# Two-layer hybrid decoder on one core: rotary queries copied to unit stride, masks moved off TensorE, some divisions on ScalarE, a new order

## The chip, the core and the metric

The kernel runs on one core of a Trainium2 chip. The core has five engines with a queue each: TensorE (PE, with its weight loads shown apart as PEld), VectorE (DVE), ScalarE (ACT), GpSimd (POOL) and SyncE (SP, which here only starts DMAs). TensorE reads SBUF and writes the eight banks of PSUM; VectorE and ScalarE read both; GpSimd works on SBUF only. The engines run side by side and wait for one another on semaphores, and each takes its own queue strictly in the order in which the program was written.

The metric is the device time of one execution in microseconds. Three runs of the kernel before gave 275.26, 276.06 and 277.32 us, so the median is 276.06 us.

## The reference

Two layers work on `x`, 256 tokens of 1024 features in float32. Each normalises `x`, projects it to ten groups of columns, runs three kinds of heads, gates their outputs and projects them back:

```python
h = rms_norm(x, norm_g[layer])
proj = jnp.einsum('btd,dc->btc', h, w_in[layer])
sb_q, sb_k, sb_v, sb_g, mb_q, mb_k, mb_v, mb_g, mem_q, mem_g = jnp.split(proj, split_at, axis=-1)
o_sb  = stick_breaking_attention(sb_q, sb_k, sb_v) * silu(sb_g)      # 6 heads of 64
o_mb  = moba_attention(rotary(mb_q), rotary(mb_k), mb_v) * silu(mb_g) # 6 heads of 64
o_mem = memory_attention(mem_q, mk, mv) * silu(mem_g)                # 4 heads, 256 memory tokens
x = x + concat[o_sb, o_mb, o_mem] @ w_out[layer]
```

A stick-breaking head weighs key s for query t by `sigmoid(z_ts) * prod_{s<j<t} (1 - sigmoid(z_tj))` over strictly earlier keys. With 256 tokens the "moba" heads have a single block, so they are causal softmax attention after a rotary turn of the first 16 of 64 dimensions. The memory heads are softmax attention without a mask. A last `rms_norm` ends the program.

## The kernel before, in words

**Projections.** Every large product is made from three products of parts: a weight `raw` is split into `hi` (the value rounded to the type that TensorE reads quickly) and `lo = raw - hi`, and the activations likewise (`T`, `mxhi`, `mxlo`). The weights arrive in 111 chunks, 768 columns wide in the main, in five `raw` buffers; a chunk is turned into `hi` (L256 on ScalarE, now and then L277 on VectorE) and `lo` (L262 on VectorE), with seven buffers of each. SyncE starts the load of a chunk when the `lo` of five chunks before is written, so a late VectorE also means late loads.

**Heads.** Scores are plain float32 products on 64 rows, two heads side by side (`pair_scores`). The tiles are named `sb_q`, `sb_k`, `mem_q`, `mem_k`, and `uT` for the rotary heads: their queries lie in `uT[:, 0:3]`, their keys in `uT[:, 3:6]`. Rotary queries and keys are produced with tokens on the partitions, turned by four small VectorE operations (`rope_task`), transposed in 32x32 blocks on VectorE (`rope_turn`, L820) and then sent through DRAM and back (`trip`: one DMA `Z<-D`, four DMAs back), which finishes the transposition. The block transposition of the queries writes them so that in `uT` neighbouring query columns of one head pair stand six elements apart; the keys stand in runs of 32.

In `pair_scores` a causal mask is added on TensorE: after the scores of a stick-breaking or a rotary pair, the product of an identity (`identb`, bf16) with a table of 0 and -1e30 (`masks`, bf16) is accumulated into the two diagonal blocks of each head. `setup` makes both on GpSimd from a constant.

A stick-breaking head (`sb_head`) then takes a tanh on ScalarE, turns it into 1 - sigmoid (L258 ACT or L684 DVE), runs a scan over the keys from the last to the first (L687, multiply, then a maximum with a `carry` that holds the start value at the block borders), and multiplies (L266). A softmax head (`soft_head`) takes the row maximum of two regions from PSUM on VectorE (L702), the exponential with its sum from PSUM on ScalarE, a reciprocal (L711) and a division (L270), both on VectorE. All heads go through a block transposition (L732) and a trip, and `pair_task` multiplies them with the values on TensorE.

**What sets the order.** No engine order is written by hand. A planner in the kernel (`Sched`) holds tasks with a priority, an estimated cost of each operation and an estimated time at which each result is ready, and always issues the operation that can start earliest, by priority within a slack. `SCAN` is its estimate of the scan in ns per element; `URG` says how many chunks ahead of TensorE a `hi` or `lo` becomes urgent; `HOLD`, `SPARE2` steer how score products are gathered and how many PSUM banks they must leave free; `ORDER` is the order of the pieces of the projection in each layer.

Of the kernel before, what the change touches and what calls it, by code (L numbers as in the profile page):

```python
# [9 lines left out]
BF = mybir.dt.bfloat16  # L10
AF = mybir.ActivationFunctionType
OP = mybir.AluOpType
# [4 lines left out]
D = 1024  # L17
# [15 lines left out]
P_H0 = -8  # L33
P_RX = 1
P_M0 = 12
P_RM = 4
P_M1 = 4
URG = 2
X67_AT = 5
CST_AT = 6  # L40
X0_AT = 7
# [4 lines left out]
DMA_GBS_1K = 300.0  # L46
TRIP_LAT = 1500.0
MEM_AT = 1
ORDER = (["sb_qk", "mb_q", "mb_k", "mk", "mv", "mem_q", "mb_v", "sb_v", "mb_g", "sb_g", "mem_g"],
         ["mv", "mk", "mb_k", "mb_q", "sb_k", "sb_q", "sb_v", "mb_g", "mem_q", "mb_v", "sb_g", "mem_g"])  # L50
GATES = {"sb_g": 3, "mb_g": 3, "mem_g": 2}
HOLD = 6000.0
SPARE2 = 2
DVE_HI = 400.0
SLACK_PE = 60.0
SLACK = 120.0


# [141 lines left out]
def hybrid_trunk(ctx: ExitStack, tc: tile.TileContext, x, mem, norm_g, w_in, w_mem_kv, w_out,  # L200
# [12 lines left out]
        return ap.tensor.name.startswith("bank")  # L213

    mode = {"m": None}

    def pe_mode(m):

# [49 lines left out]

    def ts(out, a, s, op=OP.mult):
        nc.vector.tensor_scalar(out, a, s, None, op0=op)  # L270
        S.op("dve", 1.0417 * _free(out) + 65.0)

    def copy(out, in_, eng):
        if eng == "act":
# [13 lines left out]
    xs = sb("xs", [128, 2, D])  # L288
    cst = sb("cst", [128, 512])
    gc = sb("gc", [128, 32])  # L290
    identb = sb("identb", [128, 128], BF)
    masks = sb("masks", [128, 2, 128], BF)
    negone = sb("negone", [128, 128])
    junk = sb("junk", [128, 512], BF)
    gb = sb("gb", [128, D])
# [100 lines left out]
    def dma_chunk(now=0.0, q=None):  # L396
        j = prog["dma"]
        if j >= len(chunks):
            return
        p, kk, c, w = chunks[j]  # L400
        n = len(kk)
        dma(raws[j % RAW][:, :n * w].rearrange("p (k c) -> p k c", c=w),
            p.src[:, kk[0]:kk[0] + n, c:c + w], ("raw", j), q, now)
        prog["dma"] += 1
        if j == X67_AT:
            load_xT(6, 8, now=now)
        for t, at in enumerate((X0_AT, X1_AT)):
            if j == at:
                dma(xs[:, t, :], x_r[:, t, :], ("x", t), now=now)
        if j == CST_AT:  # L410
            dma(cst, consts[:, 0:512], "cst", now=now)
            dma(S.res["w"].items[0][2][:, :256], consts[:, 512:768], "msk", now=now)

    def hi_task():
        for j, (p, kk, _, w) in enumerate(chunks):
# [42 lines left out]
    def setup():  # L458
        yield R("pool")
        nc.gpsimd.memset(negone, -1.0)  # L460
        S.op("pool", 2400.0)
        S.mark("setup0")
        yield R("pool", need=["cst", "msk"])
        m = S.res["w"].items[0][2][:, :256]
        nc.gpsimd.tensor_copy(identb, ident)
        nc.gpsimd.tensor_copy(masks, m.rearrange("p (m c) -> p m c", m=2))
        nc.gpsimd.memset(carry, 0.0)
        nc.gpsimd.memset(carry[:, 128:129], 0.5)
        for _, _, a in S.res["a"].items:
            nc.gpsimd.memset(a[:, 384:385], 0.5)  # L470
        S.op("pool", 2400.0)
        S.mark("setup")

# [170 lines left out]
    def pair_scores(l, kind, c):  # L644


        qn, kn = {"sb": ("sb_q", "sb_k"), "mem": ("mem_q", "mk"), "mb": ("mb_q", "mb_k")}[kind]
        _, sc = yield R("pe", need=["setup", (qn, l, c), (kn, l, c)], alloc=["bank", "bank"],
                      spare=3, spare2=SPARE2, form="row")
        if kind == "mem":  # L650
            regs = [(slice(0, 256), slice(0, 128), slice(0, 256)), (slice(256, 512), slice(128, 256), slice(0, 256))]
        else:
            regs = [(slice(0, 128), slice(0, 128), slice(0, 128)), (slice(128, 384), slice(128, 256), slice(0, 256))]
        st, mv_ = qs[kind], ks[kind]
        for j, (o, a, b) in enumerate(regs):
            for h in range(2):
                r = slice(h * 64, h * 64 + 64)
                lhsT, rhs, out = st[r, c, a], mv_[r, c, b], sc[h][:, o]
                if kind == "mb":
                    lhsT = st.rearrange("p c x -> p (c x)").rearrange("p (n m) -> p m n", m=6)[r, 3 * j + c]  # L660
                    rhs = mv_.rearrange("p c x -> p (c x)").rearrange("p (i t c a) -> p c t i a", i=4, t=2, c=3)[r, c, 0:1 + j]
                    out = out.rearrange("p (t i a) -> p t i a", i=4, a=32)
                mm(out, lhsT, rhs, j == 0, kind == "mem" and j == 1)
        if kind != "mem":
            yield R("pe")
            for h in range(2):
                for j, o in enumerate((slice(0, 128), slice(256, 384))):
                    mm(sc[h][:, o], identb, masks[:, 0 if kind == "sb" else 1, :], False, j == 1)
        for h in range(2):
            S.mark(("qkdone", l, kind, 2 * c + h))  # L670
            scs[l, kind, 2 * c + h] = sc[h]

    def sb_head(l, h):


# [4 lines left out]
        e, (a,) = yield R(("act", 413.0), ("dve", 265.0), alloc=["a"])  # L680
        if e == "act":
            act(a[:, 0:384], w, AF.Copy, scale=-0.5, bias=0.5)
        else:
            nc.vector.tensor_scalar(a[:, 0:384], w, -0.5, 0.5, op0=OP.mult, op1=OP.add)  # L684
            S.op("dve", 0.52 * 384 + 65.0)
        yield R("dve")
        nc.vector.tensor_tensor_scan(a[:, 383::-1], a[:, 383::-1], carry[:, ::-1], 0.5, op0=OP.mult, op1=OP.max)  # L687
        S.op("dve", SCAN * 384 + 70.0)
        yield R("dve")
        stt(w, w, 1.0, a[:, 1:385], OP.add, OP.mult)  # L690
        S.free("a", a)
        S.mark(("w", l, "sb", h))
        ws[l, "sb", h] = w

    def soft_head(l, h, kind):
        mb = kind == "mb"
        first = 0 if mb else 3
        reg = [(0, 128), (128, 384)] if mb else [(0, 256), (256, 512)]
        _, (st,) = yield R("dve", alloc=["st"], need=[("qkdone", l, kind, h)])
        sc = scs.pop((l, kind, h))  # L700
        for t, (r0, r1) in enumerate(reg):
            nc.vector.tensor_reduce(st[:, t:t + 1], sc[:, r0:r1], axis=AX.X, op=OP.max, negate=True)  # L702
            S.op("dve", 1.0417 * (r1 - r0) + 65.0)
            if t == 0:
                yield R("dve")
        _, (w,) = yield R("act", alloc=["w"], cond=lambda: 5 * l + first + h // 2 <= turn["w"] + 1)
        for t, (r0, r1) in enumerate(reg):
            act(w[:, r0:r1], sc[:, r0:r1], AF.Exp, bias=st[:, t:t + 1], accum_out=st[:, 2 + t:3 + t])
        S.free("bank", sc)
        yield R("dve")  # L710
        nc.vector.reciprocal(st[:, 0:2], st[:, 2:4])  # L711
        S.op("dve", 81.0)
        yield R("dve")
        for t, (r0, r1) in enumerate(reg):
            ts(w[:, r0:r1], w[:, r0:r1], st[:, t:t + 1])
        S.free("st", st)
        S.mark(("w", l, kind, h))
        ws[l, kind, h] = w

    def pair_turn(l, kind, c):  # L720
# [5 lines left out]
        for b in range(2):  # L726
# [6 lines left out]
            S.op("dve", 1.0417 * n * 128 + 65.0)  # L733
            S.free("wT" if kind == "sb" else "w", w)
        if kind != "sb":
            turn["w"] += 1
# [72 lines left out]
    def rope_turn(l, name):  # L809

        D = None
        for t in range(2):
            _, bufs = yield R("dve", need=[("rope", l, name, t)], alloc=[] if t else ["D"])
            D = D or bufs[0]
            rn = ropes.pop((l, name, t))
            if name == "mb_q":
                o = D[:, :768].rearrange("p (j r m) -> p m j r", j=4, r=32)[:, t * 3:t * 3 + 3]
            else:
                o = D[:, :768].rearrange("p (j m r) -> p m j r", j=4, r=32)[:, t * 3:t * 3 + 3]
            nc.vector.transpose(o, rn[0].rearrange("p (m j r) -> p m j r", j=4, r=32))  # L820
            S.op("dve", 465.0)
            S.free("rn", rn)
        A = (qs if name == "mb_q" else ks)["mb"].rearrange("p c x -> p (c x)")
        yield from trip(D, A, 192, ("trip", l, name), need=[("mT", l, k) for k in range(KT)])
        for c in range(3):
            S.ready[name, l, c] = S.ready["trip", l, name]

    def trip(D, F, e, name, need=(), alloc=()):

# [81 lines left out]
    def main():  # L911
# [26 lines left out]
        for l in range(DEPTH):  # L938
# [33 lines left out]

            S.spawn(set_table(l), 0)
            for h in range(SBH):
                S.spawn(sb_head(l, h), 10 + h)
            for h in range(MEMH):
                S.spawn(soft_head(l, h, "mem"), 30 + h)
            for h in range(SBH):
                S.spawn(soft_head(l, h, "mb"), 20 + h)
            for p0, kind, n in ((8, "sb", 3), (18, "mb", 3), (28, "mem", 2)):  # L980
# [142 lines left out]
```

## Time and profile before

| What | Before |
|---|---|
| median of three runs | 276.06 us (275.26 to 277.32) |
| the profiled execution's own time | 278.56 us |
| its span in the trace | 276.8 us |
| mean granted TensorE clock | 0.994 of full |
| PE, PEld busy | 267.0 us, 239.6 us |
| DVE busy | 229.1 us |
| ACT busy | 171.2 us |
| POOL busy | 3.7 us, 14 instructions |
| bytes moved by DMA | 66.80 MB, 241 GB/s |

The page gives one execution of the program; times are in microseconds unless marked ns. A row of a group reads: line, engine, operation, output <- inputs, partitions x elements, count, then busy time in us, mean duration in ns of one, and the idle time of the engine before them with what ended it. Matmuls overlap their neighbours, so the mean duration of one is longer than the distance from its start to the next; what a block of matmuls costs is read from the stretch between two starts. A float32 score product appears twice in the trace, as two passes.

### The profile page before, as it was taken

Reading aid. Unit: us, or ns where it says so; the run is one execution under the profiler, and the core shown is the slowest. Engines: PE = TensorE matmul, PEld = TensorE weight load, DVE = VectorE, ACT = ScalarE, POOL = GpSimd, SP = SyncE. Lnnn points to the kernel's source line nnn. Section 1 sums busy time; section 2 is a strip of 40 time slices with the busy share of each in tenths; the row PEclk is TensorE's granted clock in tenths of the full one; section 3 lists DMA queues with packets and bytes.
Section 4 is the critical chain, followed back from the end, with each engine's and each line's share of the span. In section 5 each row is a group of like instructions: output and inputs, shape, how many; then the busy total and the mean of one; then the engine's idle time right before and its main releaser. Section 6 shows DMA issues by size and latency. Waiting matters only on the chain.

```text
span 276.8 us, 4954 instructions
## 1 busy us (share of the span) xinstructions
PE 267.0 (96%) x1685; PEld 239.6 (87%) x1685; DVE 229.1 (83%) x504; ACT 171.2 (62%) x378; POOL 3.7 (1%) x14
## 2 busy tenths in 40 slices
PE   7999999999998999999999999999999999999991
PEld 3989999988896888889999999888988898898990
DVE  3954999999997899897878679559999999995482
ACT  4888769954776476492866446446558467664152
POOL 0020000000000000000000000000000000000000
PEclk9999999999999999999999999999999999999997
DMA  7999767989998989967386867783478997798003
GB/s 236 393 407 345 275 206 228 304 259 282 364 308 240 263 270 274 280 209 220 99 286 184 290 187 223 238 267 115 145 236 285 220 347 196 287 266 266 2 0 152
DMA packets 51193, 66.80 MB, mean 241 GB/s; under 512 B 3936, under 2 KB 46560, under 8 KB 51168
## 3 DMA queue, kind: packets, MB, share of 16 engines
q1 hardware_dynamic: 50448, 64.91, 74.5%
q0 software_dynamic: 288, 1.05, 1.0%
q10 hardware_dynamic: 432, 0.52, 0.6%
q8 instruction: 13, 0.21, 0.3%
q14 instruction: 12, 0.10, 0.1%
HBM read 57.03 MB, written 9.44 MB: 240 GB/s over the span
## 4 chain that ended last, share of the span: by engine, by line
PE 86%; DMA 4%; DVE 4%; ACT 3%; issue 1%; ACTq 0%; DVEq 0%
PE bank L232 85%; DMA raw<-in_w_in_dram 3%; DVE lo L262 2%; DMA uT<-xT_dram 1%; DVE a L687 1%; PE bank L237 1%; DVE xs L262 0%; ACT wT L258 0%; ACT hi L256 0%; DVE D L732 0%; ACT w L258 0%; DVE wT L266 0%; ACT junk L258 0%; DVE w L266 0%; DVE mem_q L266 0%
## 5 line engine op out<-in xcount | busy, mean ns | idle before, releaser
L262 DVE TENSOR_TENSOR lo<-raw,hi 128x768 fp32r<-128x768 f32 (+2 forms) x111 | 101.2, 919 | 9.1 <-ACT hi L256 8.3
L232 PE MATMUL bank<-T,hi 128*128 128x512 f32 (+1 forms) x294 | 101.7, 404 | 0.9 <-ACT T L258 0.9
L256 ACT CAST hi<-raw 128x768 fp32r<-128x768 f32 (+2 forms) x106 | 84.3, 812 | 27.6 <-DMA raw<-in_w_in_dram 10.0
L232 PE MATMUL bank<-hi,T 128*128 128x384 f32 (+1 forms) x320 | 77.8, 328 | 0.0
L232 PE MATMUL bank<-T,lo 128*128 128x256 f32 x288 | 73.7, 285 | 0.0
L232 PEld LDWEIGHTS bank<-T,hi 128*128 128x128 f32 x294 | 54.5, 196 | 12.5 <-ACT T L258 1.8
L232 PEld LDWEIGHTS bank<-hi,T 128*128 128x128 f32 x320 | 55.8, 188 | 1.0 <-issue 0.7
L232 PEld LDWEIGHTS bank<-T,lo 128*128 128x128 f32 x288 | 53.8, 192 | 3.3 <-DVE lo L262 0.6
L232 PE MATMUL bank<-lo,T 128*128 128x384 f32 (+1 forms) x160 | 52.0, 325 | 0.3 <-DVE lo L262 0.3
L232 PE MATMUL bank<-hi,mxhi 128*128 128x384 f32 (+1 forms) x96 | 30.7, 320 | 0.0
L232 PEld LDWEIGHTS bank<-lo,T 128*128 128x128 f32 x160 | 30.1, 188 | 0.7 <-DVE lo L262 0.7
L232 PE MATMUL bank<-lo,mxhi 128*128 128x384 f32 (+1 forms) x96 | 30.5, 317 | 0.0
L232 PE MATMUL bank<-hi,mxlo 128*128 128x384 f32 (+1 forms) x96 | 30.5, 317 | 0.0
L232 PEld LDWEIGHTS bank<-hi,mxhi 128*128 128x128 f32 x96 | 18.1, 189 | 0.8 <-issue 0.8
L232 PEld LDWEIGHTS bank<-hi,mxlo 128*128 128x128 f32 x96 | 18.1, 189 | 0.1
L232 PEld LDWEIGHTS bank<-lo,mxhi 128*128 128x128 f32 x96 | 18.1, 189 | 0.0
L258 ACT ACTIVATE junk<-xs 128x384 bf16<-128x384 f32 (+2 forms) x16 | 8.4, 522 | 15.7 <-DVE xs L262 14.9
L258 ACT ACTIVATE w<-bank,st 128x256 f32<-128x256 f32 (+1 forms) x40 | 17.2, 454 | 0.8 <-DVE st L702 0.8
L702 DVE TENSOR_REDUCE st<-bank 128x1 f32<-128x256 f32 (+1 forms) x40 | 13.2, 368 | 0.0
L258 ACT ACTIVATE T<-uT,gc 128x256 fp32r<-128x256 f32 x24 | 11.3, 501 | 2.7 <-DMA uT<-xT_dram 2.7
L732 DVE STREAM_TRANSPOSE D<-w 128x384 f32<-128x384 f32 (+1 forms) x20 | 12.4, 624 | 0.0
L258 ACT ACTIVATE gT<-bank 128x256 f32<-128x256 f32 x16 | 6.1, 384 | 9.7 <-PE bank L232 9.7
(101 smaller groups left out, 270.0 us busy)
## 6 DMA issues: line engine op xcount, KB each, us to landing
raw<-in_w_in_dram SPq DMA_DIRECT2D x71, 384.0 KB, 4.7
raw<-in_w_out_dram SPq DMA_DIRECT2D x20, 384.0 KB, 4.9
Z<-D SPq DMA_DIRECT2D x16, 384.0 KB, 4.6
raw<-in_w_mem_kv_dram SPq DMA_DIRECT2D x8, 384.0 KB, 4.0
F<-Z SPq DMA_DIRECT2D x24, 96.0 KB, 5.3
T<-Z SPq DMA_DIRECT2D x24, 96.0 KB, 4.8
uT<-memT_dram SPq DMA_DIRECT2D x8, 256.0 KB, 4.7
Z<-D SPq DMA_DIRECT2D x4, 512.0 KB, 5.4
```

Source lines behind the costliest of these rows:

```text
L232: nc.tensor.matmul(out, lhsT=lhsT, rhs=rhs, start=start, stop=stop, **kw)
L237: nc.tensor.transpose(out, in_, idt)
L256: nc.scalar.copy(out, in_)
L258: nc.scalar.activation(out, in_, func, **kw)
L262: nc.vector.tensor_tensor(out, a, b, op=op)
L687: nc.vector.tensor_tensor_scan(a[:, 383::-1], a[:, 383::-1], carry[:, ::-1], 0.5, op0=OP.mult, op1=OP.max)
L702: nc.vector.tensor_reduce(st[:, t:t + 1], sc[:, r0:r1], axis=AX.X, op=OP.max, negate=True)
L732: nc.vector.transpose(o, w[:, :n * 128].rearrange("p (m j r) -> p m j r", j=4, r=32))
```

## The change

Six things are done together.

- Rotary queries come back from their trip into a free buffer `F`, and one copy of 768 columns (on ScalarE or VectorE, as the planner finds) puts them into `uT` with neighbouring columns next to each other. Their block transposition now writes the same layout as that of the keys.
- The mask products are gone. For stick-breaking heads GpSimd sets the masked part of the two diagonal blocks to 1 (`affine_select`, L684) between the 1 - sigmoid step and the scan, and the scan is turned round in sign (minimum with a negative `carry`).
- For rotary heads the row maximum pass becomes one operation that subtracts the scores from a mask table in SBUF (`causal`), writes the result to `w` and takes its minimum (L710); the exponential then reads `w` in SBUF with a scale of -1, and the PSUM bank is free after the VectorE pass.
- A division of a softmax head may also go to ScalarE.
- `setup` no longer waits for the constants, and the mask table is loaded straight into `causal`.
- Priorities, costs and the order of pieces are new: `ORDER`, `SCAN`, `URG`, `HOLD`, `SPARE2`, the priorities of the head groups, and costs of some VectorE operations.

```diff
-SCAN = 1.1
+SCAN = 2.065
...
-URG = 2
+URG = 1
...
-        _, sc = yield R("pe", need=["setup", (qn, l, c), (kn, l, c)], alloc=["bank", "bank"],
+        _, sc = yield R("pe", need=[(qn, l, c), (kn, l, c)], alloc=["bank", "bank"],
...
-                    lhsT = st.rearrange("p c x -> p (c x)").rearrange("p (n m) -> p m n", m=6)[r, 3 * j + c]
+                    lhsT = st.rearrange("p c x -> p (c x)").rearrange("p (m n) -> p m n", m=6)[r, 3 * j + c]
...
-        if kind != "mem":
-            yield R("pe")
-            for h in range(2):
-                for j, o in enumerate((slice(0, 128), slice(256, 384))):
-                    mm(sc[h][:, o], identb, masks[:, 0 if kind == "sb" else 1, :], False, j == 1)
...
-            act(a[:, 0:384], w, AF.Copy, scale=-0.5, bias=0.5)
+            act(w, w, AF.Copy, scale=-0.5, bias=0.5)
...
+        yield R("pool", need=["setup"])
+        own = w.rearrange("p (t c) -> p t c", c=128)[:, 0:3:2]
+        nc.gpsimd.affine_select(out=own, in_=own, pattern=[[0, 2], [-1, 128]], compare_op=OP.is_gt, fill=1.0,
+                                base=0, channel_multiplier=1)
+        S.op("pool", 700.0)
+        _, (a,) = yield R("dve", alloc=["a"])
+        nc.vector.tensor_tensor_scan(a[:, 383::-1], w[:, ::-1], carry[:, ::-1], -1.0, op0=OP.mult, op1=OP.min)
...
-            nc.vector.tensor_reduce(st[:, t:t + 1], sc[:, r0:r1], axis=AX.X, op=OP.max, negate=True)
+            if mb:
+                nc.vector.tensor_tensor_reduce(bufs[1][:, r0:r1], sc[:, r0:r1], causal[:, 256 - r1 + r0:256], -1.0, 3e38,
+                                               OP.add, OP.min, st[:, t:t + 1])
+            else:
+                nc.vector.tensor_reduce(st[:, t:t + 1], sc[:, r0:r1], axis=AX.X, op=OP.max, negate=True)
...
-        yield R("dve")
+        n = reg[1][1]
+        e, _ = yield R(("act", 0.833 * n + 240.0), ("dve", 0.52 * n + 260.0))
         for t, (r0, r1) in enumerate(reg):
-            ts(w[:, r0:r1], w[:, r0:r1], st[:, t:t + 1])
+            if e == "act":
+                act(w[:, r0:r1], w[:, r0:r1], AF.Copy, scale=st[:, t:t + 1])
+            else:
+                ts(w[:, r0:r1], w[:, r0:r1], st[:, t:t + 1])
...
+        if name == "mb_q":
+            F = yield from trip(D, None, 192, ("trip", l, name), alloc=["Fs"])
+            e, _ = yield R(("act", 700.0), ("dve", 460.0), need=[("trip", l, name)] + free)
+            src = F[:, :768].rearrange("p (i m r) -> p m i r", i=4, r=32)
+            copy(qs["mb"].rearrange("p c x -> p (c x)").rearrange("p (m i r) -> p m i r", m=6, i=4), src, e)
+            S.free("Fs", F)
```

By the built programs, the move shows at three places.

On TensorE, layer 0, the end of the rotary scores (`uT`) and what follows. In the kernel before, the third pair is followed by twelve loads of `identb` and twelve mask products, of which the first rows stand here:

```order
L232 MATMUL bank_109<-uT 128x256
L232 MATMUL bank_107<-uT 128x256
L232 LDWEIGHTS identb
L232 MATMUL bank_112<-masks,identb 128x128
L232 LDWEIGHTS identb
L232 MATMUL bank_112<-masks,identb 128x128
L232 LDWEIGHTS identb
L232 MATMUL bank_113<-masks,identb 128x128
```

In the changed kernel the projection of the memory keys goes on at once:

```order
L236 MATMUL bank_112<-uT 128x256
L236 MATMUL bank_106<-uT 128x256
L236 MATMUL bank_107<-T_73,hi_98 128x512
L236 MATMUL bank_107<-T_73,lo_105 128x256
L236 MATMUL bank_107<-T_73,hi_98 128x512
```

All 48 mask products and their 48 loads are gone from TensorE's queue, and nothing has come in their place.

On VectorE, layer 0, around the first rotary heads. `st` holds the row maxima and sums, `lo` is a weight chunk's low part. Before, the maxima of the six heads stand in a run, with the first divisions (L270) behind them:

```order
L732 STREAM_TRANSPOSE D_131<-wT_125 128x3x4x32
L702 TENSOR_REDUCE st_148<-bank_112 128x1
L702 TENSOR_REDUCE st_149<-bank_113 128x1
L702 TENSOR_REDUCE st_148<-bank_112 128x1
L702 TENSOR_REDUCE st_149<-bank_113 128x1
L702 TENSOR_REDUCE st_150<-bank_108 128x1
L702 TENSOR_REDUCE st_151<-bank_114 128x1
```

Now the copy of the rotary queries comes first, with scans and transpositions of stick-breaking heads behind it, and each masked pass is two instructions (the pass, and one that writes its minimum), with `lo` between them:

```order
L282 COPY uT<-F_122 128x768
L270 SCALAR_TENSOR_TENSOR wT_128<-wT_128,a_115 128x384
L688 SCALAR_TENSOR_TENSOR a_116<-wT_124,carry 128x384
L755 STREAM_TRANSPOSE D_130<-wT_128 128x3x4x32
L270 SCALAR_TENSOR_TENSOR wT_124<-wT_124,a_116 128x384
L710 ISA w_117,st_147<-bank_109,causal 128x128
L710 ISA st_147 128x1
L755 STREAM_TRANSPOSE D_130<-wT_124 128x3x4x32
L266 TENSOR_TENSOR lo_99<-raw_90,hi_92 128x768
L710 ISA w_117,st_147<-bank_109,causal 128x256
L710 ISA st_147 128x1
```

The 24 maxima of rotary heads have become 24 passes and 24 writes, all on VectorE; over the whole program 17 of the 28 divisions of 256 columns and 5 of the 12 of 128 have left VectorE for ScalarE.

On GpSimd, from the end of `setup`, in the changed kernel. `gb` is the row of norm gains, `wT` a stick-breaking head:

```order
L471 MEMSET a_116 128x1
L459 DMA gb<-in_norm_g_dram 128x1024
L684 ISA
L684 AFFINE_SELECT wT_124<-wT_124 128x2x128
L684 AFFINE_SELECT wT_125<-wT_125 128x2x128
L684 AFFINE_SELECT wT_126<-wT_126 128x2x128
```

GpSimd had nothing but the two loads of `gb` after its setup; now twelve selects, six to a layer, stand behind and between them, and VectorE's scans wait for these.

More of the change, by code (lines that the diff above doesn't have):

```diff
@@ L26 @@
         "mem_q": (3072, 256), "mem_g": (3328, 256)}
-SCAN = 1.1
+SCAN = 2.065
+PR_SB = [8, 18]
+PR_MB = [18, 18]
+PR_MEM = [28, 28]
 TANH = ([("ln", "x", 0), ("ln", "x", 1), ("ln", "mem", 0), ("ln", "mem", 1)], [("ln", 0, 0), ("ln", 0, 1)])
@@ L48 @@
 MEM_AT = 1
-ORDER = (["sb_qk", "mb_q", "mb_k", "mk", "mv", "mem_q", "mb_v", "sb_v", "mb_g", "sb_g", "mem_g"],
-         ["mv", "mk", "mb_k", "mb_q", "sb_k", "sb_q", "sb_v", "mb_g", "mem_q", "mb_v", "sb_g", "mem_g"])
+ORDER = (["sb_qk", "mb_k", "mb_q", "mem_q", "mv", "mb_v", "mk", "sb_v", "mb_g", "sb_g", "mem_g"],
+         ["mk", "mv", "mb_k", "mb_q", "mb_g", "sb_k", "sb_q", "sb_v", "mem_q", "mb_v", "sb_g", "mem_g"])
 GATES = {"sb_g": 3, "mb_g": 3, "mem_g": 2}
[L52 to L55, printed above, removed]
+HOLD = 8000.0
+SPARE2 = 0
+DVE_HI = 800.0
+SLACK_PE = 120.0
 SLACK = 120.0
@@ L270, in ts @@
         nc.vector.tensor_scalar(out, a, s, None, op0=op)
-        S.op("dve", 1.0417 * _free(out) + 65.0)
+        fast = 0.52 if not is_psum(a) else 1.0417
+        S.op("dve", fast * _free(out) + (65.0 if isinstance(s, float) else 130.0))
     def copy(out, in_, eng):
@@ L290, in hybrid_trunk @@
     gc = sb("gc", [128, 32])
-    identb = sb("identb", [128, 128], BF)
-    masks = sb("masks", [128, 2, 128], BF)
+    causal = sb("causal", [128, 256])
     negone = sb("negone", [128, 128])
@@ L411, in dma_chunk @@
             dma(cst, consts[:, 0:512], "cst", now=now)
-            dma(S.res["w"].items[0][2][:, :256], consts[:, 512:768], "msk", now=now)
+            dma(causal[:, 128:256], consts[:, 640:768], "msk", now=now)
     def hi_task():
@@ L462, in setup @@
         S.mark("setup0")
[L463 to L466, printed above, removed]
+        nc.gpsimd.memset(causal[:, 0:128], 0.0)
         nc.gpsimd.memset(carry, 0.0)
-        nc.gpsimd.memset(carry[:, 128:129], 0.5)
+        nc.gpsimd.memset(carry[:, 128:129], -1.0)
         for _, _, a in S.res["a"].items:
-            nc.gpsimd.memset(a[:, 384:385], 0.5)
+            nc.gpsimd.memset(a[:, 384:385], -1.0)
         S.op("pool", 2400.0)
@@ L705, in soft_head @@
                 yield R("dve")
-        _, (w,) = yield R("act", alloc=["w"], cond=lambda: 5 * l + first + h // 2 <= turn["w"] + 1)
+        if mb:
+            w = src = bufs[1]
+            S.free("bank", sc)
+            yield R("act")
+        else:
+            _, (w,) = yield R("act", alloc=["w"], cond=turn_at)
+            src = sc
         for t, (r0, r1) in enumerate(reg):
-            act(w[:, r0:r1], sc[:, r0:r1], AF.Exp, bias=st[:, t:t + 1], accum_out=st[:, 2 + t:3 + t])
-        S.free("bank", sc)
+            act(w[:, r0:r1], src[:, r0:r1], AF.Exp, scale=-1.0 if mb else 1.0, bias=st[:, t:t + 1],
+                accum_out=st[:, 2 + t:3 + t])
+        if not mb:
+            S.free("bank", sc)
         yield R("dve")
@@ L815, in rope_turn @@
             rn = ropes.pop((l, name, t))
[L816 to L819, printed above, removed]
+            o = D[:, :768].rearrange("p (j m r) -> p m j r", j=4, r=32)[:, t * 3:t * 3 + 3]
             nc.vector.transpose(o, rn[0].rearrange("p (m j r) -> p m j r", j=4, r=32))
-            S.op("dve", 465.0)
+            S.op("dve", 660.0)
             S.free("rn", rn)
[L823 to L826, printed above, removed]
+        free = [("mT", l, k) for k in range(KT)]
+        if name == "mb_q":
[4 more added lines that the diff above has]
+            S.free("Fs", F)
+            for c in range(3):
+                S.mark((name, l, c))
+        else:
+            yield from trip(D, ks["mb"].rearrange("p c x -> p (c x)"), 192, ("trip", l, name), need=free)
+            for c in range(3):
+                S.ready[name, l, c] = S.ready["trip", l, name]
     def trip(D, F, e, name, need=(), alloc=()):
```

31 lines of the change are left out of this document (18 added, 13 removed).

## The prediction

> **What bounds the kernel now.** I read the page's shares first, then the busy times by stage, then who kept TensorE waiting.
>
> ```profile
> span 276.8 us, 4954 instructions
> PE 267.0 (96%) x1685; PEld 239.6 (87%) x1685; DVE 229.1 (83%) x504; ACT 171.2 (62%) x378; POOL 3.7 (1%) x14
> PE 86%; DMA 4%; DVE 4%; ACT 3%; issue 1%; ACTq 0%; DVEq 0%
> ```
>
> TensorE is busy nearly throughout, and 86% of the chain that ended last is its own work. The columns of the next view are start and end, length, then busy time and count for PE, PEld, DVE, ACT and POOL.
>
> ```profile
> 25.00:66.00 41.00, 40.65 (x268) 37.85 (x268) 40.28 (x93) 29.84 (x64) 0.66 (x1) 1.00 0.82 261
> 66.00:90.00 24.00, 22.98 (x156) 20.94 (x156) 22.09 (x60) 16.02 (x49) 0.00 (x0) 1.00 0.96 308
> 205.00:255.00 50.00, 50.00 (x315) 43.24 (x315) 45.29 (x110) 30.27 (x74) 0.00 (x0) 1.00 0.91 273
> 271.00:277.00 6.00, 0.00 (x0) 0.00 (x0) 1.16 (x3) 1.62 (x5) 0.00 (x0) 0.70 0.46 175
> ```
>
> In layer 1 (205 to 255) TensorE has no gap at all. After 271 it has nothing left: these 6.0 us are the last normalisation and the output, which the change leaves as they are. The first line matters most: in layer 0 VectorE is as full as TensorE (40.28 of 41.00, then 22.09 of 24.00, together 62.4 of 65.0), so what is added to VectorE there can become a wait. TensorE's waits after the start are few:
>
> ```profile
> PE bank L232 <- ACT sb_v L258: 1.0, 1, 1.0
> PE bank L232 <- DVE lo L262: 0.3, 1, 0.3
> PE bank L237 <- DVE w L266: 0.2, 1, 0.2
> ```
>
> That is 1.5 us. A better order of the same work can give no more than these; less work on TensorE gives its own length, if VectorE keeps up.
>
> **The change part by part.**
>
> *Mask products and the stride of the queries.* Both are read from the stretches between the start of one block on TensorE and the start of the next.
>
> ```profile
> 34.06:36.23 2.17, 2.17 (x25) 1.00 0.00 0
> 36.23:36.88 0.65, 0.65 (x14) 1.00 0.24 52
> 65.70:68.75 3.05, 3.05 (x25) 1.00 1.08 360
> 68.75:69.41 0.66, 0.66 (x15) 1.00 1.03 257
> 184.88:186.40 1.52, 1.52 (x18) 1.00 1.01 275
> 186.40:186.83 0.43, 0.43 (x11) 1.00 0.37 102
> 189.79:190.89 1.10, 1.10 (x10) 1.00 0.12 34
> 190.89:191.54 0.65, 0.65 (x10) 1.00 0.85 250
> 191.54:192.54 1.00, 1.00 (x11) 1.00 0.55 194
> 192.54:193.19 0.65, 0.65 (x15) 1.00 0.00 0
> 200.65:201.85 1.20, 1.20 (x10) 1.00 0.57 165
> 201.85:202.05 0.20, 0.20 (x6) 1.00 0.64 196
> ```
>
> Lines 2, 4, 6, 10 and 12 are the mask products: 0.65 + 0.66 + 0.43 + 0.65 + 0.20 = 2.59 us for all 48. They go, and on TensorE nothing replaces them: **-2.6**. Lines 3, 7, 9 and 11 are the rotary scores, 3.05 + 1.10 + 1.00 + 1.20 = 6.35 us for six head pairs. Lines 1, 5 and 8 are the stick-breaking scores, of the same shapes and number, whose queries lie at unit stride: 2.17 + 1.52 + 0.65 = 4.34. The weight loads tell why:
>
> ```profile
> L232 PEld LDWEIGHTS bank<-uT 64*128 64x128 f32 x48 | 5.7, 309 | 0.7 <-ACT a L258 0.2 <-ACT hi L256 0.2 <-issue 0.2
> L232 PEld LDWEIGHTS bank<-sb_k,sb_q 64*128 64x128 f32 x48 | 3.5, 187 | 0.7 <-DVE sb_q L266 0.3 <-DVE sb_k L266 0.2
> ```
>
> 309 against 187 ns for one load is 122 x 48 = 5.9 us, and half of it, 2.9, if the two heads of a pair load side by side. The bounds are 0 (if the gap comes from the keys in runs of 32, which stay) and 2.9; the difference of the blocks is 6.35 - 4.34 = 2.0, which lies between, and I take that: **-2.0**. Blocks of scores and of values are interrupted about as often as before, so nothing is counted for that.
>
> *VectorE.*
>
> ```profile
> L702 DVE TENSOR_REDUCE st<-bank 128x1 f32<-128x256 f32 x28 | 10.7, 408 | 0.0
> L702 DVE TENSOR_REDUCE st<-bank 128x1 f32<-128x128 f32 x12 | 3.1, 275 | 0.0
> L262 DVE TENSOR_TENSOR ev<-bank,gT 128x256 f32<-128x256 f32 x16 | 6.4, 413 | 0.0
> L687 DVE TENSOR_TENSOR_SCAN a<-a,carry 128x384 f32<-128x384 f32 x12 | 11.3, 946 | 0.0
> L529 DVE TENSOR_SCALAR ss<-ss 128x1 f32<-128x1 f32 x12 | 2.0, 164 | 0.5 <-ACT junk L258 0.4
> L270 DVE TENSOR_SCALAR w<-w,st 128x256 f32<-128x256 f32 x28 | 9.0, 347 | 0.0
> L270 DVE TENSOR_SCALAR w<-w,st 128x128 f32<-128x128 f32 x12 | 3.3, 275 | 0.0
> L277 DVE CAST hi<-raw 128x768 fp32r<-128x768 f32 x4 | 2.2, 560 | 1.6 <-PE bank L232 1.0 <-DMA raw<-in_w_in_dram 0.4
> L258 ACT ACTIVATION_READ_ACCUMULATOR w<-bank,st 128x1 f32 x40 | 8.7, 218 | 0.0
> ```
>
> The masked maximum is not in the trace. From below it costs what the plain maximum does (408 and 275 ns); from above what a scan does, 946 / 384 = 2.46 ns per element, so 630 and 315: 0.26 us more for a head. Nearest is a pass over a bank and an SBUF tile, 413 for 256: no dearer than now. New is the write of the minimum behind each pass, 24 of them: between 0 (hidden) and 218 ns (what ScalarE takes to read an accumulator); I take the smallest VectorE operation, 164, so 24 x 0.164 = +3.9 us. Of the divisions 17 x 0.347 + 5 x 0.275 = 7.3 us leave. VectorE ends some 3.4 us lighter over the program, but not evenly. In layer 0 before 90 us it gains 12 writes (2.0) and the copy of the queries (a cast of 768 took 0.56), and loses by the new order the divisions of two rotary heads (2 x 0.62): +1.3 against 2.6 us of idle time. It just fits. I count **0** for layer 0: TensorE's waits there, 1.3 of the 1.5 us, are VectorE's and `sb_v`'s already, and I expect them back in other places. The end of the range is 12 x 0.218 + 6 x 0.26 + 0.56 - 1.24 = +3.5, 0.9 beyond the idle time. In layer 1 VectorE has 50.0 - 45.3 = 4.7 us to spare and more divisions leave: 0.
>
> *ScalarE* takes 22 divisions. A scaled copy from SBUF took 501 ns:
>
> ```profile
> L258 ACT ACTIVATE T<-uT,gc 128x256 fp32r<-128x256 f32 x24 | 11.3, 501 | 2.7 <-DMA uT<-xT_dram 2.7
> ```
>
> At most 22 x 0.5 = 11 us on 171 of 277. What is queued behind a division are `hi` casts, and a head's transposition waits for it; at 66% load both have cover, and without it each wait is one such operation, 0.5 us. The exponential from SBUF instead of PSUM is the same operation and counted even.
>
> *GpSimd.* The selects are not in the trace. Nearest rows:
>
> ```profile
> L466 POOL CAST masks<-w 128x256 bf16<-128x256 f32 x1 | 1.1, 1125 | 0.0
> L467 POOL MEMSET carry<- 128x384 f32 x1 | 0.4, 413 | 0.0
> 13.40 1.05 DVE L262 TENSOR_TENSOR lo<-raw,hi 128x768 fp32r<-128x768 f32 x1
> ```
>
> A select of 256 columns lies between a memset of 384 (413 ns) and a cast of 256 (1125 ns, as its input is read). I take the upper one. The scan on VectorE now waits for it, and behind a waiting scan stand `lo` passes that TensorE needs. The other half of a head's chain (tanh, 1 - sigmoid) runs a head or two ahead on ScalarE, so with six selects in some 15 us of VectorE work the wait has cover: 0. Without it, 1.1 us for each layer's first head. The cast ran beside the third row here, a `lo` of 1.05 us, where a full one took
>
> ```profile
> L262 DVE TENSOR_TENSOR lo<-raw,hi 128x768 fp32r<-128x768 f32 x99 | 93.4, 951 | 9.1 <-ACT hi L256 8.3 <-DMA uT<-Z 0.6
> ```
>
> so a meeting cost VectorE 0.1 us; twelve cost 1.2, and 0.6 in a layer is within the idle time. By the Trainium skill (page "SBUF — State Buffer", section "Who interferes with whom") a VectorE instruction with two SBUF inputs and a GpSimd instruction that reads SBUF exclude each other through a shared port, and whoever comes second waits for the whole of the first. The row fits that as well as it fits sharing, since the `lo` came first and the long cast may have been the one that waited.
>
> *The trip of the queries* now goes to `F` and is copied on. In layer 0 the planner puts the queries behind the keys, and their return DMAs behind two weight loads on SyncE, each of which waits for a `lo`:
>
> ```profile
> F<-Z SPq DMA_DIRECT2D x24, 96.0 KB, 5.3
> uT<-Z SPq DMA_DIRECT2D x16, 96.0 KB, 4.4
> ```
>
> The return takes 0.9 us more if it lands like an `F`, and 0.56 for the copy. Before, the rotary scores began at 65.70, as the last `uT` came in. Now memory queries and values stand between, as filler. I take 0, and 1.5 us late as the bound.
>
> **The rivals.**
>
> *VectorE becomes the bound in layer 0.* For it: 40.28 of 41.00. TensorE gets 0.65 + 0.66 + 1.0 (half of 2.0) = 2.3 us shorter there and VectorE no shorter. Then these 2.3 are lost, and with the dear end of the pass and its write 0.9 more: the program gains 2.3 or 1.4, 273.8 to 274.7 us by the median. Against it: VectorE's work may slide to behind 90 us.
>
> *GpSimd and VectorE lock each other out: slower.* If a select holds VectorE for its length, at 1.125 us twelve cost 13.5: 6.75 in layer 0, where nothing is to spare, and 6.75 - 4.7 = 2.0 in layer 1. 8.8 - 4.6 = +4.2: 280.3 us. It decides from the select at which 12 s - 4.7 - 4.6 exceeds 2.8 (1%), s = 1.0 us. Against it: only a select that comes first holds VectorE up, and 413 ns would be harmless. The page named above states such a lock.
>
> *The order also removes TensorE's waits.* The scan is now planned at about 2 ns per element, and it took 2.46; before, the plan said 1.1. All 1.5 us gone: 276.06 - 6.1 = 270.0.
>
> *Unit stride does not help* and only the masks count: 276.06 - 2.6 = 273.5.
>
> **How the numbers follow.** The profiled execution's own time is 278.56 us, its span 276.8 and 1.8 around it. -2.6 - 2.0 = -4.6 makes 274.0 for it. It ran 2.5 us above the median of the three runs, 276.06; taken from the median, 276.06 - 4.6 = **271.5 us**, 1.7% less. Chances: this forecast 0.53, VectorE as the bound 0.20, waits gone 0.14, lock 0.08, no help from the stride 0.05. What can be told from no change is about 1%, so faster means under 273.3. Of the forecast 0.50 lies there, and 0.02 of the last case; with the waits gone that is 0.66. Slower: the lock and a little of the second case, 0.09. The rest, 0.25, is within 1%. The range takes in the loads at their 2.9 with the waits gone, 276.06 - 2.6 - 2.9 - 1.5 = 269.1, a little rounded, up to 276, where the second case has met the late queries too; it leaves out the lock and tails, under 2 in 10. The forecast's own range is 270.5 to 273.3.
>
> **What would show it.** Right: loads of `uT` at about 187 ns, rotary score blocks of some 0.72 us for a pair, no `masks`, TensorE ending about 4.6 us earlier with its waits near 1.5, and 6.0 us behind it. Wrong: TensorE waiting on `lo` or on the `uT` copy between 60 and 90 us (second case), scans of 0.95 us or `lo` passes stretched while a select runs (lock), a longer write behind the masked pass, or `uT` loads still near 309.

## The result, and the profile after

The changed kernel took 274.13 us (median of 20 runs, 271.76 to 278.91), the kernel before beside it 277.48 us (20 runs, 274.57 to 279.90; the three runs known at first gave 276.06). The ratio is 0.9885, with a 95% interval of 0.9859 to 0.9910: 3.2 us faster (2.5 to 3.9), where 4.6 were forecast. Ratios here leave out the slow runs of a kernel (over 1.5% above its fastest), so they need not be the quotient of two medians, and the profiled execution of the changed kernel, 276.39 us, is one of these slow runs. Its span is 274.2 us; before it was 276.8, in an execution of 278.56 us.

The page of the changed kernel, its shares and the chain of waits by engine:

```profile
span 274.2 us, 4883 instructions
PE 263.4 (96%) x1637; PEld 235.2 (86%) x1637; DVE 224.0 (82%) x503; ACT 183.7 (67%) x405; POOL 9.1 (3%) x25
PE 53%; DMA 22%; DVE 8%; issue 7%; ACT 5%; SPq 2%; POOL 1%; POOLq 0%; DVEq 0%; ACTq 0%
```

TensorE is again busy 96% of the span, but of the chain that ended last it holds 53% where it held 86%; 22% are transfers now (4% before). The same stages as in the prediction, for the changed kernel (busy time and count of PE, PEld, DVE, ACT, POOL, then granted clock, DMA share, GB/s):

```profile
25.00:66.00 41.00, 40.50 (x254) 37.49 (x253) 39.11 (x91) 30.95 (x63) 3.90 (x7) 1.00 0.81 252
66.00:90.00 24.00, 24.00 (x159) 20.47 (x158) 23.47 (x70) 19.26 (x54) 0.00 (x0) 1.00 0.97 311
205.00:255.00 50.00, 48.88 (x310) 42.57 (x308) 42.38 (x91) 32.18 (x73) 0.55 (x1) 1.00 0.97 273
255.00:271.00 16.00, 13.20 (x90) 12.99 (x90) 10.66 (x26) 6.56 (x20) 0.00 (x0) 1.00 0.09 34
```

TensorE ends at 255 + 13.2 = 268.2 us instead of 270.7: 2.5 us earlier in these two executions. In layer 1 (205 to 255) it had no gap before; now it has 1.1 us of them, with the DMA share up from 0.91 to 0.97. Who it waited for, in the list of waits:

```profile
PE bank L236 <- DMA T<-Z: 1.9, 2, 1.1
PE bank L236 <- DVE lo L266: 0.4, 2, 0.2
PEld bank L236 <- DVE lo L266: 2.7, 7, 0.6
```

The columns are the sum, the number and the longest. The wait for `sb_v` is gone; weight loads wait for `lo` longer than before (2.7 us; it was 1.3). New are two waits for `T<-Z`, the way back of a softmax pair's trip: 0.8 us near 98 and 1.1 near 253, where the values of the last memory heads are multiplied. What the change's own operations cost:

```profile
L236 PEld LDWEIGHTS bank<-uT 64*128 64x128 f32 x48 | 3.7, 187 | 1.0 <-ACT uT L260 0.7 <-DVE wT L270 0.2
L710 DVE CUSTOM_DVE_ANT_0 w<-bank,causal 128x256 f32<-128x256 f32 x12 | 4.7, 414 | 0.0
L710 DVE CUSTOM_DVE_ANT_0 w<-bank,causal 128x128 f32<-128x128 f32 x12 | 3.1, 277 | 0.3 <-PE bank L236 0.3
L710 DVE DVE_READ_ACCUMULATOR2_ANT st<- 128x1 f32 x24 | 2.0, 84 | 0.0
```

and the selects by their line, with the shortest, the median and the longest in ns:

```profile
L684 POOL TENSOR_SCALAR_AFFINE_SELECT wT<-wT x12: 400/422/1089, 50.7 to 204.8; 128x256 f32<-128x256 f32 x12
```

The blocks of rotary scores on TensorE, from start to start:

```profile
66.31:68.48 2.17, 2.17 (x25) 1.00 0.90 349
189.33:190.75 1.42, 1.42 (x17) 1.00 0.98 301
191.40:192.22 0.82, 0.82 (x11) 1.00 0.12 43
```

Together 4.41 us instead of 6.35.

### The profile page after: what moved, and what is told of

The parts are those of the page before. It is cut to its first block, busy times and chain, and to the rows that moved or that the text cites. A ratio compares the mean times of both kernels' runs of the same rounds, so it can differ in the third digit from the quotient of the medians.

```text
span 274.2 us, 4883 instructions
## 1 busy us (share of the span) xinstructions
PE 263.4 (96%) x1637; PEld 235.2 (86%) x1637; DVE 224.0 (82%) x503; ACT 183.7 (67%) x405; POOL 9.1 (3%) x25
## 4 chain that ended last, share of the span: by engine, by line
PE 53%; DMA 22%; DVE 8%; issue 7%; ACT 5%; SPq 2%; POOL 1%; POOLq 0%; DVEq 0%; ACTq 0%
PE bank L236 53%; DMA T<-Z 5%; DMA F<-Z 5%; DMA raw<-in_w_out_dram 4%; DVE lo L266 3%; DMA Z<-D 3%; DMA raw<-in_w_in_dram 3%; ACT hi L260 2%; DMA gb<-in_mem_dram 1%; DMA uT<-xT_dram 1%; SPq L871 1%; DVE a L688 1%; POOL wT L684 1%; SPq L346 1%; ACT T L262 1%
## 5 line engine op out<-in xcount | busy, mean ns | idle before, releaser
L260 ACT CAST hi<-raw 128x768 fp32r<-128x768 f32 (+2 forms) x110 | 88.0, 812 | 35.0 <-DMA raw<-in_w_in_dram 13.1
L262 ACT ACTIVATE w<-w,st 128x256 f32<-128x256 f32 (+1 forms) x46 | 20.0, 463 | 2.7 <-DVE st L730 1.6
L270 DVE SCALAR_TENSOR_TENSOR gT<-ga,gT 128x256 f32<-128x256 f32 x16 | 6.7, 417 | 7.1 <-ACT ga L262 7.0
L270 DVE SCALAR_TENSOR_TENSOR T<-uT,gc,T 128x256 fp32r<-128x256 f32 x24 | 11.3, 479 | 0.8 <-ACT T L262 0.8
```

Of the source, the lines that this page charges most:

```text
L260: nc.scalar.copy(out, in_)
L262: nc.scalar.activation(out, in_, func, **kw)
L270: nc.vector.scalar_tensor_tensor(out, a, s, b, op0=op0, op1=op1)
```

## The experiments

Where an edit says that the planner's costs stay, all queues are the same row for row except for what is named. Otherwise the planner orders the work anew. Times are set against the kernel before, run on the same chip in the same job.

**The changed kernel again.** No edit.

> The changed kernel once more, for a second trace and as the base of the three kernels beside it. Theory A (TensorE's work shrank by the 4.5 us that were forecast, but the transposition trips of the last memory heads in layer 1 land no earlier than before, so TensorE now waits for them): again about 1.2% under the kernel before, and again a wait for T<-Z of 1 to 1.5 us near 252 us. Theory B (the selects on GpSimd and VectorE's short passes hold up lo in layer 0): the waits for lo near 57 to 62 us, 1 us in the first trace, are at least as long as the wait for T<-Z. Theory C (the waits differ from execution to execution and have no fixed place): another trace shows them elsewhere.

Six runs, 271.49 to 278.76 us; ratio 0.9837 (0.9771 to 0.9903), too wide to sharpen the result. In its trace there is a single wait for `T<-Z` of 1.2 us, near 99, and nearly none near 253; `lo` has 0.9 us on the matmuls' side instead of 0.4. So the sum of the waits returns, and their places do so in part. Theory A's wait near 252 us is missing here, but it stands in two other traces of nearly the same kernel, 0.9 us without the selects and 1.1 us with ten idle products at the start. So neither A nor C holds alone.

**The saving on TensorE alone, in the kernel before.**

```diff
-                    lhsT = ....rearrange("p (n m) -> p m n", m=6)[r, 3 * j + c]
+                    lhsT = ....rearrange("p (m n) -> p m n", m=6)[r, 3 * j + c]
...
-                    mm(sc[h][:, o], identb, masks[:, ...], False, j == 1)
+                    S.op("pe", 128 * 0.44 + pe_mode((128, 128)))   # planner's cost only
```

> The kernel before with TensorE's saving alone: the 48 mask products are left out and the rotary queries are read at unit stride from the tile as it lies. So no causal mask is applied and the query columns are taken in another sequence. The planner is told the old costs, and the queues of all other engines stay as they were, row for row. The sum of TensorE's own work says -4.5 us (2.6 masks, 1.9 loads), 1.6%. Theory A: the saving comes less than whole, since trips and weight loads do not get shorter: 2.5 to 4 us, with a new wait for a DMA in the layers' ends. If the whole 4.5 us come, the loss in the changed kernel is due to what it adds or to its order, not to trips as such.

277.45 us, ratio 1.0033 (1.0001 to 1.0065): some 4.2 us of TensorE's work gone (2.6 of mask products, 1.6 of rotary blocks in this trace), and nothing gained. Every theory missed this. In layer 1 VectorE takes it. VectorE's time line of the kernel before, at the place in layer 1 where the rotary maxima (L702) and then `lo` follow the last scan (start, length):

```profile
201.25 0.57 DVE L732 STREAM_TRANSPOSE D<-wT 128x384 f32<-128x384 f32 x1
201.74 1.12 DVE L702 TENSOR_REDUCE st<-bank 128x1 f32<-128x256 f32 x4
202.77 0.94 DVE L262 TENSOR_TENSOR lo<-raw,hi 128x768 fp32r<-128x768 f32 x1
```

and of this kernel:

```profile
201.95 1.11 DVE L702 TENSOR_REDUCE st<-bank 128x1 f32<-128x256 f32 x4
202.99 0.94 DVE L262 TENSOR_TENSOR lo<-raw,hi 128x768 fp32r<-128x768 f32 x1
```

with this line in its list of waits from 190 to 204 us:

```profile
PE bank L232 <- DVE lo L262: 1.4, 1, 1.4
```

Before, this `lo` ended at 203.72 and TensorE began its first product with it at 203.77, 0.05 us later: no wait is listed, yet there was nothing to spare. Now TensorE is there earlier and waits 1.4 us, and `lo` comes no sooner.

In layer 0 it is something else. At 48 us TensorE waits 1.1 us for a bank that a tanh on ScalarE still reads. Ahead of the tanh ScalarE has a `hi` cast. In the kernel before, and in this one, this cast stands here:

```profile
45.89 0.82 ACT L256 CAST hi<-raw 128x768 fp32r<-128x768 f32 x1
```

```profile
45.90 0.83 ACT L256 CAST hi<-raw 128x768 fp32r<-128x768 f32 x1 [1.32 <-DMA raw<-in_w_in_dram]
```

The bracket gives the idle time ahead of it and what ended it: ScalarE now waits for the weight load. SyncE started that load 0.9 us earlier than before (39.89 instead of 40.81 us), and the cast still begins at the same time. It is the same at 86 us: the load started at 79.53 instead of 79.86, the cast behind it at 86.04 instead of 86.08, and TensorE's wait for `sb_v`, which follows on ScalarE, grows from 1.0 to 1.5 us. From 66 to 90 us the transfers take 0.99 of the DMA engines' time (0.96 before). So in layer 0 the saving is lost to weight loads that land no sooner. The wait at 143 (the normalisation) has grown too. Product for product TensorE is level with the kernel before at 88 us and 0.2 us behind it from 204 us to its end.

**The changed kernel without its selects.**

```diff
-        nc.gpsimd.affine_select(out=own, in_=own, ...)
```

> The changed kernel without the twelve selects on GpSimd: the stick-breaking heads are not masked. The planner's costs stay, and all other queues are the same row for row. VectorE's operations beside a select were up to 0.2 us longer in the trace, 0.9 us in all, half of it in layer 0. Theory A: 0 to -0.5 us against the changed kernel. Theory B: -1 us or more, and the lo waits between 57 and 62 us go.

273.32 us, ratio 0.9879 (0.9840 to 0.9918), the same as with them. The selects and what they do to VectorE cost nothing that can be measured, though the two intervals leave room for 1 us. The traces agree: from the start of the 113th product to its end TensorE took 243.0 us here and 243.1 with the selects. Its products' waits for `lo` in layer 0 (0.4 us) are gone without any gain, so nothing speaks for theory B.

**The last memory values later in TensorE's queue.**

```diff
+        if l == 1 and kind == "mem" and c == 1:
+            S.ready["F", l, kind, c] += 2500.0
```

The kernel that ran told the planner 2.5 us, and the products stand 15 output products later (2.6 us); the expectation was written for 1.5 us and 9.

> The changed kernel with the planner told that the trip of the last memory pair of layer 1 takes 1.5 us more, which puts the last two value products 9 output products later in TensorE's queue (about 1.6 us) and changes nearly nothing else. Theory A: the 1.4 us wait for T<-Z shrinks to under 0.3, and the time by 0.8 to 1.3 us, unless the gated memory heads then come late for the rest of the output product, which would give up to 0.8 back. Theories B and C: within 0.3 us of the changed kernel.

274.78 us, ratio 0.9932 (0.9895 to 0.9969): no better than the changed kernel. The wait for `T<-Z` near 253 is gone; in its place TensorE's weight loads wait for `mxhi` and `mxlo` of these heads (0.6 and 0.5 us), and near 108 its products wait for an `ev` (0.8). The wait moved on along the same chain, as the last part of the expectation allowed.

**The saving taken back in the changed kernel.**

```diff
-                    lhsT = ....rearrange("p (m n) -> p m n", m=6)[r, 3 * j + c]
+                    lhsT = ....rearrange("p (n m) -> p m n", m=6)[r, 3 * j + c]
...
+        if kind != "mem":
+            for h in range(2):
+                for j, o in enumerate((slice(0, 128), slice(256, 384))):
+                    nc.tensor.matmul(sc[h][:, o], lhsT=zeros, rhs=zeros, start=False, stop=j == 1)
```

> The changed kernel with TensorE's saving taken back and nothing else: 48 products of zeros of the size of the mask products behind the same scores, and the queries read six elements apart again, so that the query columns come in another sequence. All other queues stay row for row. It follows on the kernel before, where the saving alone gave nothing. Theory D (in both kernels the sequence of lo passes, heads and weight loads on VectorE, ScalarE and the DMAs sets the pace, and TensorE has some slack at many short waits): less than 1.5 us slower than the changed kernel. Theory E (with the new order and the lighter VectorE TensorE is the bound): the whole 4.5 us slower, which is about the time of the kernel before or 1 us over it.

280.38 us, ratio 1.0098 (1.0059 to 1.0137), 2.1% over the changed kernel or 6 us. The work put back was more than 4.5: from start to start the zero products took 3.4 us in all, the rotary scores 2.8 more, the stick-breaking scores 0.8 more, together 7.0. Six of the seven reach the end. Here theory E holds: in the changed kernel TensorE's work is on the path.

**All divisions on VectorE, planned anew.**

```diff
-        e, _ = yield R(("act", 0.833 * n + 240.0), ("dve", 0.52 * n + 260.0))
+        e, _ = yield R("dve")
```

> The changed kernel with all divisions on VectorE: 22 passes, 7.3 us by the old rows, come back to VectorE and leave ScalarE; the planner places them anew. Theory D: VectorE sets the pace in layer 0, so some 2 to 4 us slower than the changed kernel. Theory E: TensorE has the bound, VectorE has room, under 1 us slower.

292.00 us, ratio 1.0510 (1.0466 to 1.0555), far beyond both expectations. Its waits for trips (sum, number, longest), and TensorE around the longest (busy time and count, granted clock, DMA share, GB/s):

```profile
PE bank L236 <- DMA T<-Z: 5.1, 3, 3.4
```

```profile
125.00:130.00 5.00, 5.00 (x30) 0.97 0.72 229
135.00:140.00 5.00, 1.61 (x10) 0.89 0.40 99
140.00:145.00 5.00, 5.00 (x17) 0.50 0.00 0
```

A wait of 3.4 us costs itself, and then TensorE runs at half its clock for 5 us: 17 products where 30 stood. Near 120 and near 262 us the clock falls as well, to 0.69 and 0.68 over 5 us.

**The old operations in the new order**, with `ORDER`, `SCAN`, `URG`, `HOLD`, `SPARE2`, the planner's other constants, the priorities and the cost estimates of the changed kernel in the kernel before, **and the new operations in the old order**, the reverse.

> The kernel before with the new order alone: the new sequence of pieces, priorities, estimates and limits, but with the mask products on TensorE, strided queries, plain maxima, and divisions on VectorE only. Theory D: the order is the larger part of the gain, so 1 to 3 us faster than the kernel before. Theory E: the order alone gives nothing, and within 1 us of the kernel before, since its 4.5 us of work on TensorE are still there.

> The changed kernel's operations (no masks on TensorE, unit stride, masked maximum pass, selects, divisions on either engine) with the old sequence of pieces, priorities, estimates and limits. If the operations carry the gain, it is within 1 us of the changed kernel; if the order does, it is about as slow as the kernel before (within 1 us); if both are needed together, both this and the kernel before with the new order stay at the time of the kernel before.

296.99 us (ratio 1.0667, 1.0623 to 1.0712) and 287.27 us (1.0334, 1.0288 to 1.0380). Both are far slower than either kernel, which none of the theories said. Each trace has a long wait of TensorE at the end of layer 0, of 3.5 and of 3.8 us, and a lower clock behind it. So the constants fit only the operations for which they were chosen. What the order as such is worth can't be read from these two, since each also is a bad plan.

**The kernel before without its divisions, with and without TensorE's saving.** In the first kernel the line below is the only edit; in the second it joins the edit of the saving alone.

```diff
-            ts(w[:, r0:r1], w[:, r0:r1], st[:, t:t + 1])
+            S.op("dve", 1.0417 * (r1 - r0) + 65.0)   # planner's cost only
```

> The kernel before without its 40 divisions (the softmax heads stay unnormalised); 13 us leave VectorE, spread over both layers, and nothing is added anywhere. All other queues are the same row for row. With the next run and the two of before (as it is, and with the saving on TensorE) this makes a square: saving or not, lighter VectorE or not. If TensorE's work is a bound beside VectorE's (theory F), a lighter VectorE alone gives little, 0 to -2 us against the kernel before.

> The kernel before with both: the 48 mask products left out and the queries read at unit stride, and the 40 divisions left out; the queues otherwise row for row as before. Theory F (TensorE and VectorE are both full in this order, so that each saving alone is eaten by the other engine): -3 to -6 us against the kernel before, where the saving on TensorE alone gave +0.3%. Theory G (the saving is eaten by the order itself, that is by the places at which transfers, evacuations and passes are queued, whatever VectorE's load): within 1.5 us of the kernel before.

277.72 us (ratio 1.0001, 0.9963 to 1.0039) and 278.52 us (1.0041, 1.0007 to 1.0075). Neither helps, nor do both together, as theory G had it. With both, TensorE still waits at 49 us for the tanh (0.8 us), at 88 for `sb_v` (1.0) and at 203 for `lo` (1.5). VectorE in this kernel (busy time and count, granted clock, DMA share, GB/s):

```profile
66.00:90.00 24.00, 19.84 (x47) 1.00 0.98 317
186.00:204.00 18.00, 17.28 (x33) 1.00 0.51 161
```

and in the kernel before:

```profile
66.00:90.00 24.00, 22.09 (x60) 1.00 0.96 308
186.00:204.00 18.00, 16.87 (x33) 1.00 0.48 151
```

VectorE's busy time fell from 229.1 to 220.7 us. From 186 to 204 us no division stood; scans, transpositions and `lo` fill VectorE as before, and `lo` comes as late. From 66 to 90 us VectorE now has 4.2 us of idle time, and TensorE passes 88 us no earlier: there VectorE isn't the bound. The weight loads are what the trace shows in its place, with ScalarE waiting for them 1.1 us at 46 and 1.8 us at 86. So the saving of TensorE is lost in layer 0 to weight loads and in layer 1 to VectorE's passes in one stretch. This is read from the traces. No run makes the loads or that stretch shorter. The start tells the same: in the first kernel's trace the first 112 products took 2.1 us less than in the kernel before, and TensorE ended only 0.9 us earlier. In the changed kernel without selects they took 2.2 us less than with them, and TensorE ended 2.2 us earlier.

**The divisions back on VectorE in the changed kernel, the order kept.**

```diff
-                act(w[:, r0:r1], w[:, r0:r1], AF.Copy, scale=st[:, t:t + 1])
+                nc.vector.tensor_scalar(w[:, r0:r1], w[:, r0:r1], st[:, t:t + 1], None, op0=OP.mult)
+                S.op("act", 0.833 * (r1 - r0) + 186.0)
```

> The changed kernel with the 22 divisions that ScalarE had been given done by VectorE at the places where they would be issued, with the planner told ScalarE's cost, so that all queues are else row for row the same. It parts the load from the order in the run with all divisions on VectorE, which was 15 us slower and planned anew. If VectorE's load was the cause there: over 5 us slower than the changed kernel. If it was the order that the planner made of it: 0 to 3 us slower.

276.67 us, ratio 1.0002 (0.9968 to 1.0036), 1.2% or 3.2 us over the changed kernel (some 2 to 4.4 by the two intervals). Its shares, and TensorE's wait:

```profile
PE 263.6 (96%) x1637; PEld 234.2 (85%) x1637; DVE 228.8 (83%) x525; ACT 176.4 (64%) x383; POOL 9.0 (3%) x25
```

```profile
PE bank L236 <- DVE lo L266: 1.8, 5, 0.6
```

VectorE holds 4.8 us more, and TensorE waits for `lo` 1.8 us instead of 0.4. That lies between the two expectations. The two traces show less of it: from the start of the 113th product to its end TensorE took 244.3 us, and 243.1 in the changed kernel. The run that was planned anew is 6.3% or 17 us over the changed kernel; some 3 of these are load and 14 the plan that came of it. By the times of the runs these 3 are the whole gain of the change.

**Ten idle products at the start.**

```diff
         for _ in range(7):
             mm(acc, junk[:, :128], junk, True, True)
+        for _ in range(3):
+            nc.tensor.matmul(acc, lhsT=junk[:, :128], rhs=junk, start=True, stop=True)
```

> The changed kernel with ten instead of seven idle products at the start, which fill the 1 to 1.3 us in which TensorE waits for the first activations (3.7 to 5.1 us). In the traces so far the first 112 matmuls took 21.7 to 22.1 us where the matmuls behind that gap ran at full speed at once, and 23.9 us where a product of 256 columns took 213 instead of 120 ns until 10.5 us. If the gap decides that: the products run at full speed by 8 us in this trace too, the spread of the runs shrinks, and the median falls by 0.5 to 1.5 us against the changed kernel. If it is chance of another kind: the same spread and no gain, or 0.3 us lost.

273.67 us, six runs from 272.61 to 274.18, ratio 0.9882 (0.9841 to 0.9923). TensorE in the changed kernel (busy time and count, granted clock, DMA share, GB/s):

```profile
4.00:7.00 3.00, 2.29 (x10) 1.00 1.01 340
9.00:11.00 2.00, 2.00 (x8) 1.00 1.06 393
```

and here:

```profile
4.00:7.00 3.00, 3.00 (x19) 1.00 1.00 340
9.00:11.00 2.00, 2.00 (x13) 1.00 1.06 365
```

In this trace the products behind the gap run at full speed from the start, 13 instead of 8 in the same 2 us. The spread is 1.6 us instead of over 7. But the kernel without selects, with seven idle products, also ran its first products at full speed in its trace, and its six runs lay within 1.4 us. So it isn't shown that the gap decides, and by the ratio this kernel isn't shown to be faster than the changed one.

## Why the prediction was right, and where it was not

The direction held, and the time lies in the wide range of 269.1 to 276. It lies outside the forecast's own range (270.5 to 273.3) and inside that of the first rival (273.8 to 274.7). Of the 2.6 us between 271.5 and 274.13, 1.4 are the base (277.48 us by 20 runs instead of 276.06 by three). The rest is the effect: -3.35 us by the medians, -3.2 by the ratio, instead of -4.6. That it came so near is in part luck: the saving that makes up the whole sum gave nothing by itself, and what let it count was put at 0.

**TensorE's own work: right.** The 48 mask products went without successor, -2.6. The loads of `uT` fell from 309 to 187 ns and the rotary blocks from 6.35 to 4.41, -1.9 where -2.0 stood. From start to start this is -4.5 us; TensorE ended 2.5 earlier, not the 4.6 that the prediction gave as its sign. So 2.0 came back, 1.1 of them as longer listed waits of TensorE's products (2.6 us instead of 1.5).

**The step that failed is "less work on TensorE gives its own length, if VectorE keeps up", with the 0 that followed for VectorE.** I took it that 1.5 us of listed waits bound what a better order can give, and that VectorE had 4.7 us to spare in layer 1. The saving alone gave nothing in the kernel before. In layer 1 VectorE delivered there with 0.05 us to spare, in a stretch that it fills, and an average over 205 to 255 didn't show the stretch from 186 to 204 ahead of it. In layer 0 weight loads landed no sooner, and they appear in no term and no rival, though the prediction's own line for 66 to 90 us has a DMA share of 0.96. A list of waits shows who was late, not who was just in time. The first rival, VectorE as the bound in layer 0, had the loss but not its place: in the old order VectorE's bound is seen in layer 1, and in layer 0 the loads hold even when VectorE has idle time. It had been priced at half of the saving; the whole was lost.

**The divisions, counted at 0, carry the result**: put back at their places they cost 3.2 us by the runs, and TensorE's work put back costs 6. Each takes away the whole gain. The parts don't add up: the runs show that the time needs both TensorE's saving and the lighter VectorE. That it also needs an order in which the two meet elsewhere is argued, not shown. What the order adds by itself stays open.

**VectorE's new passes**: the masked pass took 414 and 277 ns, as long as the plain one (408, 275), as taken. The write behind it was mis-sized: 84 ns, not 164, so 2.0 us instead of 3.9.

**The lock did not come.** A select took 400 ns at the shortest and 422 in the median, close to the 413 of the memset; I had taken the 1125 of the cast. Beside VectorE's passes it stretched to as much as 1089. Those passes stretched by up to 0.2 us: a scan that began 0.28 us before a select ended took 1.09 us instead of 0.95. Without selects the time is the same. By the Trainium skill (page "SBUF — State Buffer", section "Who interferes with whom") the port that the two share is an exclusive lock, so that the second would wait for the first. On GpSimd's side the trace comes near it: a select that began 0.1 us behind a `lo` ended 0.3 us after it and took 1089 ns. VectorE's passes were lengthened by some half of the overlap at most, and where page and trace differ the trace decides. Spans on GpSimd are rough.

**The waits gone** (all 1.5 us) did not happen: those for `sb_v` went, those for `T<-Z` came. The queries' trip, taken at 0, held TensorE up by 0.3 us at 189.

## What to carry to other kernels

A busy share of 96% on one engine doesn't say that its work sets the time. Look where another engine's result is ready just as it is needed, and compare the busy time of both, and the DMA share, in stretches of 10 to 20 us, not over a layer. When one engine waits for another, ask what that other one waited for: here a tanh stood behind a weight load. Take away one engine's work alone, with all queues kept, before counting it as gain. And a planner's constants belong to the operations they were chosen for: changed by themselves, either half of this change cost 3 to 7%.

## What the runs showed of the hardware

TensorE's clock can make a wait dearer than its length. Waits of up to 1.2 us in the two traces of the changed kernel, and of 1.4 us in the kernel before with TensorE's saving, left it at 1.00. Behind waits of 3.4 and 3.5 us it stood at 0.50 for 5 us. The length of one wait alone doesn't settle it: in the run with all divisions on VectorE the clock was 0.68 over the 5 us around a wait of 1.5 us.

At the start the speed differs from execution to execution: the first 112 products took 21.7 to 24.0 us with seven idle products, and between 4 and 10.5 us some ran at half speed while the column of the granted clock said 1.00. So traces are best compared from behind the start; before and after happen to be alike there (23.97 and 23.92 us).

The Trainium skill (page "TensorE: Matmul & The Clock Gate", section "Part 1: The HAM clock gate") states that windows of some 3.4 us, which don't begin with the program, decide: one idle window halves the clock, one busy window restores it. The waits of about 3.5 us agree. The 1.5 us wait is shorter than such a window and doesn't, by that rule alone. At the start seven idle products fill 3.0 us, with a gap of 0.6 to 1.0 us behind them; windows that begin at any time would fit the different starts, which no run here tests.
